# Finer first quarters, plain gain loads and later turns at the seams of a one-core encoder block

## Chip, cores and metric

The kernel runs on one core of a Trainium2 chip. The metric is device microseconds of one execution. TensorE multiplies, ScalarE and VectorE do elementwise work, GpSimd a few tiny instructions, and SyncE (SP) issues every load and store.

## The reference

One layer over x of 256 tokens by 1024 channels, float32, with an RMS norm before and after every part:

```
x = x + 0.5 * rmsnorm(swiglu(rmsnorm(x, ffn1_pre_g), w_gate, w_up, w_down), ffn1_post_g)
z = rmsnorm(x, mix_pre_g) @ w_in            # q,k,v,f | u,v_s | a_A,a_B
o_a = forgetting attention(q, k, v, f);  o_b = gelu(u) * (W_s LN(gelu(v_s)) + b)
x = x + rmsnorm((sigmoid(a_A)*o_a + sigmoid(a_B)*o_b) @ w_out, mix_post_g)
x = x + 0.5 * rmsnorm(swiglu(rmsnorm(x, ffn2_pre_g), ...), ffn2_post_g)
rmsnorm(x, g) = x * rsqrt(mean(x*x) + 1e-6) * g          # D = 1024, d_ff = 4096
```

## The kernel before

Tokens are two tiles of 128 (t = 0, 1). Every float32 operand is split into a rounded high part, made by a ScalarE copy, and the rest, the low part, made by a VectorE subtraction (`split`, L85 and L86). A product is three matmuls of 512 columns: high by high, high by low weight, low by high.

Weights come in quarters, 128x2048, of 1 MiB: column half c of 512, and half kh of the contraction. `load` brings one in (5 buffers), `parts_of` splits it (4 buffers for each part), `quarter` is both. A quarter and one token tile make a unit of 12 matmuls (`proj`). `section` goes quarter by quarter and uses each for both token tiles; `section_by_tile` keeps all four quarters, does tile 0 with them (4 units) and then tile 1. After each unit the generator yields, and `tick` runs what `later(n, ...)` put off for n ticks. FFN 1's first gate section, the mixer's v, gb and w_o, and FFN 2's first gate section go by tile. `fast` is a seven-product form for the later up sections.

A norm is `square_sum` (the sum of squares of each half), `rstd` (a sum with epsilon, and a power -0.5, on [128,1], both on GpSimd), `normed` (hn = x * r * g, VectorE) and `to_xT` (four TensorE transposes for each half, then a split into xT). `post_norm` takes the squares from PSUM, multiplies y by the gain (yg, VectorE, L186) and adds into x (L190); `pre_norm` squares x and returns a function that turns the tile later. The three seams are: the head, FFN 1's end into the mixer (done1, `after`, `turn_in`), and w_o into FFN 2 (wo_done, `before`). In FFN 1 token tile 0 is turned by `after` when KEEP f steps of 6 products for tile 1 are still to come, and tile 1 by `later(3, ...)` during v; in FFN 2 tile 0 is turned by `later(4, turn[0])` during w_o's tile 1, and tile 1 by `before` at the second step.

In the head 14 dummy matmuls run while x comes. `trace` and `in_order` fix the order of the listed instructions on each engine; elsewhere the framework orders each engine's queue at build time, by program order among what it reckons to be ready. Each engine then runs its queue in order, waiting on semaphores.

Of the kernel before, what the change touches and what calls it, by code (L numbers as in the profile page):

```python
# [22 lines left out]
P = 128  # L23
D = 1024
# [10 lines left out]
NB = 4  # L35
KEEP = 2
HOLD = 2
# [8 lines left out]
def block(ctx: ExitStack, tc: tile.TileContext, a: dict, out: bass.AP):  # L46
# [20 lines left out]
    x = const.tile([P, NT, D], F32, name="x")  # L67
    for t in range(NT):
        nc.sync.dma_start(out=x[:, t, :], in_=a["x"][t])
    xT = const.tile([P, KT, NT, 2, P], F32R, name="xT")  # L70

    ident = const.tile([P, P], F32, name="ident")
    power = const.tile([P, 4], F32, name="power")
    const.tile([P, 32], F32, name="pad1")
    nc.vector.memset(power, -0.5)

    def gain(name, by=D):
        g = gains.tile([P, D], F32, tag="g", name=f"g_{name}")
        for c in range(0, D, by):
            nc.sync.dma_start(out=g[:, c:c + by], in_=a[name][:, c:c + by].broadcast_to([P, by]))  # L80
        return g
# [32 lines left out]

    def quarter(src, name):

        return parts_of(load(src, name), name)

# [3 lines left out]
    def later(n, fn):  # L122
        pending.append([n, fn])
# [9 lines left out]

    def square_sum(srcs, name, vector=None):
        ms = small.tile([P, 2], F32, tag="ms", name=f"ms_{name}")
        for c, src in enumerate(srcs):
            if vector is not None and c == 1:
                junk = mid_tile([P, 512], f"junk_{name}{c}")
                vector.append(nc.vector.scalar_tensor_tensor(out=junk, in0=src, scalar=1.0 / D, in1=src, op0=ALU.mult,
                                                             op1=ALU.mult, accum_out=ms[:, c:c + 1]))  # L140
                continue
            junk = small.tile([P, 512], mybir.dt.bfloat16, tag="junk", name=f"junk_{name}{c}", bufs=1)
            nc.scalar.activation(out=junk, in_=src, func=AF.Square, scale=1.0 / 32.0, accum_out=ms[:, c:c + 1])
        return ms

    def rstd(ms, name, trace=None):
        r = small.tile([P, 1], F32, tag="r", name=f"r_{name}")
        done = [nc.gpsimd.tensor_scalar(out=r, in0=ms[:, 0:1], scalar1=ms[:, 1:2], scalar2=RMS_EPS, op0=ALU.add,  # L148
                                        op1=ALU.add),
                nc.gpsimd.tensor_tensor(out=r, in0=r, in1=power[:, 0:1], op=ALU.pow)]  # L150
        if trace is not None:
            trace.extend(done)
        return r
# [27 lines left out]
    def post_norm(t, ys, g, half, name):  # L181
        ms = square_sum(ys, f"{name}{t}")
        ygs = []
        for c in range(2):
            yg = mid_tile([P, 512], f"yg_{name}{t}{c}")
            nc.vector.scalar_tensor_tensor(out=yg, in0=ys[c], scalar=half, in1=halves(g)[c], op0=ALU.mult, op1=ALU.mult)  # L186
            ygs.append(yg)
        r = rstd(ms, f"{name}{t}")
        for xc, yg in zip(halves(x[:, t]), ygs):
            nc.vector.scalar_tensor_tensor(out=xc, in0=yg, scalar=r, in1=xc, op0=ALU.mult, op1=ALU.add)  # L190
# [30 lines left out]

    def section(src, name, done):

        for c in range(2):
            pss = [None, None]
            for kh in range(2):
                w = quarter(src[c, kh], f"{name}{c}{kh}")
                for i in range(2):
                    for t in range(NT):
                        if pss[t] is None:  # L230
                            pss[t] = bank(f"{name}{t}{c}")
                        proj(pss[t], t, w, kh, i, 2)
                    if kh == 1 and i == 1:
                        for t in range(NT):
                            done(t, c, pss[t])
                    yield

    def section_by_tile(src, name, done, first=None):

        ws = {}  # L240
        for t in range(NT):
            for c in range(2):
                for kh in range(2):
                    if (c, kh) not in ws:
                        ws[c, kh] = first if first and (c, kh) == (0, 0) else quarter(src[c, kh], f"{name}{c}{kh}")
                ps = bank(f"{name}{t}{c}")
                for kh in range(2):
                    proj(ps, t, ws[c, kh], kh, 0, 1)
                    if kh == 1:
                        done(t, c, ps)  # L250
                    yield
# [20 lines left out]
    def fast(src, name, parts, done):  # L272
# [6 lines left out]
        def lhs_s(i):  # L279
            return lambda k, xs: parts[:, i, k, xs, :]  # L280

# [53 lines left out]

    def ffn(n, quick, done, before=None, after=None, first=None):

# [42 lines left out]
        for b in range(NB):  # L380
            steps = []
            for src, kind, fn in ((gs[b], "g", gate_done(b)), (us[b], "u", up_done(b))):
                nm = f"{kind}{n}_{b}"
                if (b, kind) == (0, "g"):
                    steps.append((section_by_tile(src, nm, fn, first), 8))
                elif (b, kind) in quick:
                    steps.append((fast(src, nm, parts[0], fn), 7))
                else:
                    steps.append((section(src, nm, fn), 8))
# [3 lines left out]
            for gen, _ in steps:  # L393
                for _ in gen:
                    at += 1
                    if b == 0 and at == 2 and before:
                        before()
                    if b == 0 and at == 9 and quick:
                        parts.append(sums(f"f{n}"))
                    tick()  # L400
                    while had > 0 and gone < had * at // total:
                        f = side.pop(0)
                        down(f, 0)
                        down(f, 1)
                        gone += 1
# [135 lines left out]
    def mixer(turn_in):  # L541
# [4 lines left out]

        later(3, turn_in[1])
        kept = forget()
        run(section_by_tile(a["w_v"], "v", v_done))
        parts = sums("mx") if FASTM else None  # L550

# [101 lines left out]
    g = halves(gain("ffn1_pre_g", 512))  # L653
    nc.sync.dma_start(out=ident, in_=a["ident"])
    trace, rs = [], []
    for t in range(NT):
        ms = square_sum(halves(x[:, t]), f"f1{t}", vector=trace)
        rs.append(rstd(ms, f"f1{t}", trace))
    hn = {}

# [6 lines left out]

    norm_of(0, 0)
    norm_of(0, 1)
    norm_of(1, 0)  # L670
    norm_of(1, 1)
    raw = load(a["g1"][0][0, 0], "g1_0", 2)
    splits = []
    turn_of(0, 0)
    first = parts_of(raw, "g1_0", 2, splits)
    trace.extend(splits[0])
    turn_of(0, 1)
    trace.extend(splits[1])
    turn_of(1, 0)
    turn_of(1, 1)  # L680
    in_order(trace)
    turn, gs = {}, []
# [6 lines left out]

    ffn(1, FAST1, done1, after=lambda: turn[0](), first=first)  # L690
    turn = mixer(turn)
# [75 lines left out]
```

## Time and profile before

| what | value |
|---|---|
| median of 3 runs (lowest, highest) | 760.64 us (760.53, 761.41) |
| the profiled execution | 760.05 us, its span 758.3 us |
| granted TensorE clock, mean | 0.997 |
| busy: TensorE, VectorE, ScalarE | 739.0, 538.2, 381.4 us |
| DMA | 141.61 MB, mean 187 GB/s |

The span runs from the first to the last instruction of the profiled execution. Busy time of TensorE is modelled from the starts of pipelined matmuls.

### The profile page before, as it was taken

To read this page: it belongs to the slowest core of one execution; us is meant where nothing else is said; L and a number is where in the kernel's file an instruction comes from. 1 tells how busy PE (TensorE), PEld (TensorE's weight loads), DVE (VectorE), ACT (ScalarE), POOL (GpSimd) and SP (SyncE) were. 2 spreads that over 40 slices of the span, in tenths; PEclk is the share of its full clock that TensorE was granted. 3 is DMA by queue.
4 is the path that set the end of the run, shared out by engine and by line. 5 is a ranking of instruction groups with operands and counts; after the bars stand their busy time and mean duration, and the time that the engine had idled before them with its cause. 6 is when DMAs were issued, how large, how long until landed. Compare 5 with 4: busy or idle time off the path is not lost. (4 is left out here: it accounts for less than half of the span.)

```text
span 758.3 us, 8470 instructions
## 1 busy us (share of the span) xinstructions
PE 739.0 (97%) x3446; PEld 608.1 (80%) x3446; DVE 538.2 (71%) x516; ACT 381.4 (50%) x376; POOL 21.5 (3%) x32
## 2 busy tenths in 40 slices
PE   6999999999999999999999999899999999999996
PEld 3888888888888877888888888678888888888885
DVE  6584798689479775755486647848479958947972
ACT  5553465356355474754544434735346545644551
POOL 1000000000000020000020000300000000000000
PEclk9999999999999999999999999999999999999999
DMA  9785168338416936633427435527525842851521
GB/s 343 304 315 182 57 236 304 126 103 341 167 56 222 333 139 203 252 150 116 162 111 276 169 112 221 187 85 275 185 73 203 302 162 65 338 207 56 201 76 56
DMA packets 21974, 141.61 MB, mean 187 GB/s; under 512 B 3184, under 2 KB 3440, under 8 KB 5680
## 3 DMA queue, kind: packets, MB, share of 16 engines
q1 hardware_dynamic: 21936, 141.08, 50.6%
q8 instruction: 27, 0.44, 0.2%
q14 instruction: 11, 0.09, 0.0%
HBM read 140.02 MB, written 1.05 MB: 186 GB/s over the span
## 5 line engine op out<-in xcount | busy, mean ns | idle before, releaser
L219 PE MATMUL g<-hi_g,xT 128*128 128x512 f32 x512 | 164.7, 393 | 0.5 <-ACT hi_g L85 0.3
L352 PE MATMUL y<-hi_d,hT 128*128 128x512 f32 x512 | 147.4, 392 | 0.0
L219 PEld LDWEIGHTS g<-hi_g,xT 128*128 128x128 f32 x512 | 96.8, 189 | 21.1 <-ACT hi_g L85 1.1
L352 PEld LDWEIGHTS y<-hi_d,hT 128*128 128x128 f32 x512 | 95.7, 188 | 19.4
L86 DVE TENSOR_TENSOR lo_g<-raw_g,hi_g 128x2048 fp32r<-128x2048 f32 (+1 forms) x33 | 73.4, 2224 | 43.8 <-ACT hi_g L85 43.8
L219 PE MATMUL g<-lo_g,xT 128*128 128x512 f32 x256 | 100.4, 392 | 2.8 <-DVE lo_g L86 2.7
L86 DVE TENSOR_TENSOR lo_d<-raw_d,hi_d 128x2048 fp32r<-128x2048 f32 x32 | 73.0, 2286 | 36.9 <-ACT hi_d L85 36.9
L352 PE MATMUL y<-lo_d,hT 128*128 128x512 f32 x256 | 81.0, 392 | 0.0
L85 ACT CAST hi_g<-raw_g 128x2048 fp32r<-128x2048 f32 (+1 forms) x33 | 61.2, 1857 | 33.7 <-PE u L219 9.8
L85 ACT CAST hi_d<-raw_d 128x2048 fp32r<-128x2048 f32 x32 | 60.8, 1914 | 25.9 <-PE g L219 8.6
L219 PE MATMUL u<-hi_u,xT 128*128 128x512 f32 x192 | 60.6, 391 | 0.0
L219 PEld LDWEIGHTS g<-lo_g,xT 128*128 128x128 f32 x256 | 48.4, 189 | 13.5 <-DVE lo_g L86 3.8
L352 PEld LDWEIGHTS y<-lo_d,hT 128*128 128x128 f32 x256 | 47.8, 188 | 9.7
L291 DVE TENSOR_TENSOR raw_u<-raw_u,raw_u 128x2048 f32<-128x2048 f32 x24 | 55.0, 2292 | 0.8
L358 ACT ACTIVATE sg<-g 128x512 f32<-128x512 f32 x32 | 18.9, 598 | 65.4 <-PE g L219 65.4
L198 PE MATMUL qk<-xT,hi_qk 128*128 128x512 f32 x128 | 46.3, 403 | 0.0
L85 ACT CAST hi_u_3p<-raw_u 128x2048 fp32r<-128x2048 f32 x14 | 26.6, 1913 | 33.0 <-DVE raw_u L291 26.0
L219 PEld LDWEIGHTS u<-hi_u,xT 128*128 128x128 f32 x192 | 36.1, 188 | 7.4
L86 DVE TENSOR_TENSOR lo_u<-raw_u,hi_u 128x2048 fp32r<-128x2048 f32 x12 | 27.3, 2289 | 17.3 <-ACT hi_u L85 17.3
L86 DVE TENSOR_TENSOR lo_u_3p<-raw_u,hi_u_3p 128x2048 fp32r<-128x2048 f32 x14 | 31.9, 2288 | 9.4 <-ACT hi_u_3p L85 9.4
L219 PE MATMUL u<-lo_u,xT 128*128 128x512 f32 x96 | 37.4, 389 | 0.0
L85 ACT CAST hi_u_1p<-raw_u 128x2048 fp32r<-128x2048 f32 x14 | 26.8, 1917 | 20.1 <-DVE raw_u L291 9.5
(254 smaller groups left out, 1270.9 us busy)
## 6 DMA issues: line engine op xcount, KB each, us to landing
raw_u<-in_u SPq DMA_DIRECT2D x32, 1024.0 KB, 4.8
raw_d<-in_dn SPq DMA_DIRECT2D x32, 1024.0 KB, 4.7
raw_g<-in_g SPq DMA_DIRECT2D x31, 1024.0 KB, 4.8
raw_qk<-in_w_qk SPq DMA_DIRECT2D x8, 1024.0 KB, 5.4
raw_v<-in_w_v SPq DMA_DIRECT2D x4, 1024.0 KB, 5.2
raw_sv<-in_w_sv SPq DMA_DIRECT2D x4, 1024.0 KB, 4.7
raw_u<-in_w_u SPq DMA_DIRECT2D x4, 1024.0 KB, 4.8
raw_ga<-in_w_ga SPq DMA_DIRECT2D x4, 1024.0 KB, 4.7
```

The lines of the kernel that those rows point to most:

```text
L85: return [nc.scalar.copy(out=hi, in_=src), nc.vector.tensor_tensor(out=lo, in0=src, in1=hi.bitcast(F32), op=ALU.subtract)]
L86: nc.vector.tensor_tensor(out=lo, in0=src, in1=hi.bitcast(F32), op=ALU.subtract)]
L198: nc.tensor.matmul(ps, lhsT=hi, rhs=xT[:, k], start=k == 0, stop=False, skip_group_check=True)
L219: nc.tensor.matmul(ps, lhsT=xT[:, kh * 4 + k, t, xs, :], rhs=v, start=kh == 0 and k == 0 and q == 0, stop=kh == 1 and k == 3 and q == 2)
L291: nc.vector.tensor_tensor(out=out, in0=p, in1=q, op=ALU.add)
L352: nc.tensor.matmul(ys[t][c], lhsT=hTs[f // 4][:, f % 4, t, xs, :], rhs=w[:, c * 512:(c + 1) * 512], start=f == 0 and q == 0, stop=f == NF ...
L358: nc.scalar.activation(out=sg, in_=y, func=AF.Silu)
```

## The change

- The gains lie in memory as 128 equal rows and are loaded plainly; before, one row was spread over 128 partitions by the load.
- In the head: x's tile 0, the identity, the gain halves, then x's tile 1 are loaded; the first two quarters (c = 0, kh = 0 and 1) come and are split in four pieces each. FFN 1's first gate section is a `section`, so both quarters serve both tiles: quarter 0 for tile 0, then tile 1, with the second halves of both tiles turned (`within`) ahead of tile 1's last 6 matmuls. The written order of VectorE and ScalarE changes with it.
- Pre-norms share their squares: half 0 on ScalarE, half 1 on VectorE. Post-norms stay on ScalarE. The sum with epsilon moves from GpSimd to VectorE for all norms.
- Quarters of v and of FFN 2's first gate section are split in four pieces (loaded whole).
- Token tile 1 is turned one unit later in the mixer (ahead of its own first unit) and two units later in FFN 2 (likewise). KEEP is 1 instead of 2.
- `section` takes the banks of both tiles at once; `parts` is a list.

```diff
-KEEP = 2
+KEEP = 1
...
-    for t in range(NT):
-        nc.sync.dma_start(out=x[:, t, :], in_=a["x"][t])
+    nc.sync.dma_start(out=x[:, 0, :], in_=a["x"][0])
...
+    nc.sync.dma_start(out=ident, in_=a["ident"])
...
-            nc.sync.dma_start(out=g[:, c:c + by], in_=a[name][:, c:c + by].broadcast_to([P, by]))
+            nc.sync.dma_start(out=g[:, c:c + by], in_=a[name][:, c:c + by])
...
-    def quarter(src, name):
-
-        return parts_of(load(src, name), name)
+    def quarter(src, name, parts=1):
+
+        return parts_of(load(src, name), name, parts)
...
-    def square_sum(srcs, name, vector=None):
+    def square_sum(srcs, name, trace=None, shared=True):
...
-            if vector is not None and c == 1:
+            if shared and c == 1:
...
-        done = [nc.gpsimd.tensor_scalar(out=r, in0=ms[:, 0:1], scalar1=ms[:, 1:2], scalar2=RMS_EPS, op0=ALU.add,
+        done = [nc.vector.tensor_scalar(out=r, in0=ms[:, 0:1], scalar1=ms[:, 1:2], scalar2=RMS_EPS, op0=ALU.add,
                                         op1=ALU.add),
                 nc.gpsimd.tensor_tensor(out=r, in0=r, in1=power[:, 0:1], op=ALU.pow)]
...
-        ms = square_sum(ys, f"{name}{t}")
+        ms = square_sum(ys, f"{name}{t}", shared=False)
...
-    def section(src, name, done):
+    def section(src, name, done, first=None, within=None):
+
+
 
         for c in range(2):
-            pss = [None, None]
+            pss = [bank(f"{name}{t}{c}") for t in range(NT)]
             for kh in range(2):
-                w = quarter(src[c, kh], f"{name}{c}{kh}")
+                early = first and (c, kh) == (0, 0)
+                w = first[kh] if first and c == 0 else quarter(src[c, kh], f"{name}{c}{kh}")
                 for i in range(2):
-                    for t in range(NT):
-                        if pss[t] is None:
-                            pss[t] = bank(f"{name}{t}{c}")
-                        proj(pss[t], t, w, kh, i, 2)
+                    if early:
+                        for j in range(2):
+                            if (i, j) == (1, 1):
+                                within()
+                            proj(pss[i], i, w, kh, j, 2)
+                    else:
+                        for t in range(NT):
+                            proj(pss[t], t, w, kh, i, 2)
...
-                    steps.append((section_by_tile(src, nm, fn, first), 8))
+                    steps.append((section(src, nm, fn, first, within) if first else section_by_tile(src, nm, fn, 4), 8))
...
-                    if b == 0 and at == 2 and before:
+                    if b == 0 and at == 4 and before:
...
-        later(3, turn_in[1])
+        later(4, turn_in[1])
         kept = forget()
-        run(section_by_tile(a["w_v"], "v", v_done))
...
+        run(section_by_tile(a["w_v"], "v", v_done, 4))
...
-    norm_of(0, 0)
+    rs = []
+    for t in range(NT):
+        rs.append(rstd(square_sum(halves(x[:, t]), f"f1{t}", trace), f"f1{t}", trace))
+        norm_of(t, 0)
+    first = [parts_of(load(a["g1"][0][0, c], f"g1_0{c}", 4), f"g1_0{c}", 4, splits) for c in range(2)]
+    turn_of(0, 0)
+    trace.extend(splits[0])
+    turn_of(1, 0)
+    for i in splits[1:4]:
+        trace.extend(i)
     norm_of(0, 1)
-    norm_of(1, 0)
     norm_of(1, 1)
...
+    def within():
+        turn_of(0, 1)
+        trace.extend(splits[4])
+        turn_of(1, 1)
+        for i in splits[5:]:
+            trace.extend(i)
+        in_order(trace)
...
-        arrays[n] = np.ascontiguousarray(i[n].reshape(1, D))
+        arrays[n] = np.ascontiguousarray(np.broadcast_to(i[n].reshape(1, D), (P, D)))
```

## Rows read from the trace of the kernel before

**Rows 1.** The page, its span and its first part, busy time by engine.

```profile
span 758.3 us, 8470 instructions
...
PE 739.0 (97%) x3446; PEld 608.1 (80%) x3446; DVE 538.2 (71%) x516; ACT 381.4 (50%) x376; POOL 21.5 (3%) x32
```

**Rows 2.** Waits of TensorE over the span: total us, times, longest us.

```profile
PE tp_f L162 <- DVE hn_f L168: 4.7, 2, 3.5
PE g L219 <- DVE lo_g L86: 2.7, 2, 1.9
```

**Rows 3.** The chain that ended last, FFN 2: start us, us, work.

```profile
526.69 0.87 PE hp L373 x8
...
544.82 5.44 PE g L219 x24
```

**Rows 4.** Timeline of the head: start us, us, engine, line, operation, [idle before <-releaser].

```profile
5.75 0.69 DVE L139 SCALAR_TENSOR_TENSOR junk_f<-x 128x512 f32<-128x512 f32 x1 [0.96 <-DMA x<-in_x]
...
8.77 2.12 PE L162 MATMUL tp_f<-ident,hn_f 128*128 128x128 f32 x16 [1.88 <-DMA ident<-in_ident]
9.44 0.59 ACT L85 CAST xT<-tp_f 128x512 fp32r<-128x512 f32 x1 [2.90 <-PE tp_f L162]
10.10 0.68 DVE L86 TENSOR_TENSOR xT<-tp_f,xT 128x512 fp32r<-128x512 f32 x1
...
18.20 0.50 PE L219 MATMUL g<-lo_g,xT 128*128 128x512 f32 x1 [1.92 <-DVE lo_g L86]
```

**Rows 5.** Windows, products of L219 in the head: window, us, PE busy (instructions).

```profile
11.20:18.19 6.99, 4.08 (x13) 1.00 1.01 427
```

**Rows 6.** DMA of the first 20 us, in 40 slices of 0.5 us.

```profile
GB/s 0 0 0 123 229 360 426 393 401 303 213 246 176 270 281 327 290 393 418 467 434 442 410 459 426 393 459 410 410 442 426 442 442 410 459 393 410 475 410 410
```

**Rows 7.** Windows of the two seams, TensorE alone (instructions at the edges count too).

```profile
479.73:484.84 5.11, 3.96 (x21) 1.00 0.57 208
484.84:502.03 17.19, 13.69 (x57) 0.90 0.57 214
273.15:278.76 5.61, 4.04 (x22) 1.00 0.50 187
278.76:291.43 12.67, 12.11 (x57) 1.00 0.77 265
```

**Rows 8.** Windows behind the second transposes before FFN 2: PEclk is the granted clock.

```profile
494.00:498.00 4.00, 4.00 (x15) 3.23 (x16) 3.92 (x7) 1.17 (x2) 0.00 (x0) 0.57 0.63 250
```

**Rows 9.** Timeline of the seam from FFN 1 to the mixer, VectorE and GpSimd.

```profile
267.67 1.42 DVE L190 SCALAR_TENSOR_TENSOR x<-yg_p,r_p,x 128x512 f32<-128x512 f32 x2 [0.35 <-POOL r_p L150]
...
271.76 1.77 POOL L148 TENSOR_SCALAR r_mx<-ms_mx 128x1 f32<-128x1 f32 x1 [4.12 <-ACT junk_mx L143]
```

**Rows 10.** Timeline of the tail.

```profile
752.66 0.19 ACT L143 ACTIVATION_READ_ACCUMULATOR junk_p<-y 128x1 f32 x1
752.89 0.69 DVE L186 SCALAR_TENSOR_TENSOR yg_p<-y,g_ffn_post_g 128x512 f32<-128x512 f32 x1 [0.65 <-ACT junk_p L143]
752.96 0.30 POOL L148 TENSOR_SCALAR r_p<-ms_p 128x1 f32<-128x1 f32 x1 [9.44 <-ACT junk_p L143]
753.34 0.56 POOL L150 TENSOR_TENSOR r_p<-r_p,power 128x1 f32<-128x1 f32 x1
753.93 1.42 DVE L190 SCALAR_TENSOR_TENSOR x<-yg_p,r_p,x 128x512 f32<-128x512 f32 x2 [0.35 <-POOL r_p L150]
```

**Rows 11.** Instructions of the tile rl in the mixer: ns min/median/max.

```profile
L576 DVE TENSOR_SCALAR rl<-mv x4: 162/165/170, 378.7 to 396.8; 128x4 f32<-128x4 f32 x4
```

**Rows 12.** Timeline of the seam from the mixer to FFN 2, VectorE.

```profile
473.60 1.42 DVE L190 SCALAR_TENSOR_TENSOR x<-yg_pm,r_pm,x 128x512 f32<-128x512 f32 x2 [0.36 <-POOL r_pm L150]
...
480.14 1.42 DVE L168 SCALAR_TENSOR_TENSOR hn_f<-x,r_f,g_ffn_pre_g 128x512 f32<-128x512 f32 x2 [0.85 <-POOL r_f L150]
...
484.27 1.28 DVE L86 TENSOR_TENSOR xT<-tp_f,xT 128x512 fp32r<-128x512 f32 x2
```

**Rows 13.** Groups of VectorE by form, 468 to 500 us: count, busy us, mean ns.

```profile
L86 DVE TENSOR_TENSOR lo_g<-raw_g,hi_g 128x2048 fp32r<-128x2048 f32 x4 | 9.1, 2286 | 2.0 <-ACT hi_g L85 2.0
```

More of the change, by code (lines that the diff above doesn't have):

```diff
@@ L131, in tick @@
             e[1]()
-    def square_sum(srcs, name, vector=None):
+    def square_sum(srcs, name, trace=None, shared=True):
         ms = small.tile([P, 2], F32, tag="ms", name=f"ms_{name}")
         for c, src in enumerate(srcs):
-            if vector is not None and c == 1:
+            if shared and c == 1:
                 junk = mid_tile([P, 512], f"junk_{name}{c}")
-                vector.append(nc.vector.scalar_tensor_tensor(out=junk, in0=src, scalar=1.0 / D, in1=src, op0=ALU.mult,
-                                                             op1=ALU.mult, accum_out=ms[:, c:c + 1]))
+                done = nc.vector.scalar_tensor_tensor(out=junk, in0=src, scalar=1.0 / D, in1=src, op0=ALU.mult,
+                                                      op1=ALU.mult, accum_out=ms[:, c:c + 1])
+                if trace is not None:
+                    trace.append(done)
                 continue
@@ L236, in section, with section_by_tile @@
                     yield
-    def section_by_tile(src, name, done, first=None):
+    def section_by_tile(src, name, done, parts=1):
         ws = {}
@@ L244, in section_by_tile @@
                     if (c, kh) not in ws:
-                        ws[c, kh] = first if first and (c, kh) == (0, 0) else quarter(src[c, kh], f"{name}{c}{kh}")
+                        ws[c, kh] = quarter(src[c, kh], f"{name}{c}{kh}", parts)
                 ps = bank(f"{name}{t}{c}")
@@ L279, in lhs_s @@
         def lhs_s(i):
-            return lambda k, xs: parts[:, i, k, xs, :]
+            return lambda k, xs: parts[0][:, i, k, xs, :]
         def product(ps, lhs, raw, nm, start):
@@ L334, in block, with ffn @@
     marks = {}
-    def ffn(n, quick, done, before=None, after=None, first=None):
+    def ffn(n, quick, done, before=None, after=None, first=None, within=None):
         gs, us, dn = a[f"g{n}"], a[f"u{n}"], a[f"dn{n}"]
@@ L384, in ffn @@
                 if (b, kind) == (0, "g"):
-                    steps.append((section_by_tile(src, nm, fn, first), 8))
+                    steps.append((section(src, nm, fn, first, within) if first else section_by_tile(src, nm, fn, 4), 8))
                 elif (b, kind) in quick:
-                    steps.append((fast(src, nm, parts[0], fn), 7))
+                    steps.append((fast(src, nm, parts, fn), 7))
                 else:
@@ L545, in v_done @@
             nc.scalar.copy(out=v[:, t, c * 512:(c + 1) * 512], in_=ps)
-        later(3, turn_in[1])
+        later(4, turn_in[1])
         kept = forget()
-        run(section_by_tile(a["w_v"], "v", v_done))
-        parts = sums("mx") if FASTM else None
+        run(section_by_tile(a["w_v"], "v", v_done, 4))
+        parts = [sums("mx")] if FASTM else None
         def columns(src, name, done):
@@ L653, in block @@
     g = halves(gain("ffn1_pre_g", 512))
[L654 to L659, printed above, removed]
+    nc.sync.dma_start(out=x[:, 1, :], in_=a["x"][1])
+    trace, splits, hn = [], [], {}
     def norm_of(t, c):
@@ L666, in turn_of @@
         trace.extend(to_xT(t, c, hn[t, c], "f1"))
-    norm_of(0, 0)
+    rs = []
[8 more added lines that the diff above has]
+        trace.extend(i)
     norm_of(0, 1)
-    norm_of(1, 0)
     norm_of(1, 1)
[L672 to L681, printed above, removed]
+    def within():
[5 more added lines that the diff above has]
+        in_order(trace)
     turn, gs = {}, []
@@ L688, in done1 @@
         turn[t] = pre_norm(t, gs[1], "mx")
-    ffn(1, FAST1, done1, after=lambda: turn[0](), first=first)
+    ffn(1, FAST1, done1, after=lambda: turn[0](), first=first, within=within)
     turn = mixer(turn)
```

## The prediction

> **What bounds the kernel now.** I read the page's first part, then TensorE's waits, then the timeline around each wait. TensorE is busy for 97% of the span [rows 1], so only its gaps can be won, and they lie in few places. The waits say which [rows 2]: transposes waiting for a normed tile, and first weight halves in the head. Elsewhere TensorE issues one 512-column product every 0.2267 us (24 in 5.44) and one transpose every 0.11 us (8 in 0.87) [rows 3]. So I price each place by counting: time spent minus products times 0.2267 minus transposes times 0.11.
>
> *Head.* The 14th product starts at 18.20 [rows 4], 13 came before it [rows 5]: as if an unbroken run had begun at 18.20 - 13 x 0.2267 = 15.25. The page's DMA row dips to 176 to 303 GB/s between 4.5 and 7.5 us, when the gain rows are spread to 128 partitions, against 390 to 475 later [rows 6].
>
> *Seams.* Four stretches, two per seam, hold 8 transposes each plus 12 or 48 products, ideally 3.62 or 11.78 us [rows 7]. FFN 1 to mixer: 5.61 (one product more at its edge, 0.23) loses 1.76, 12.67 loses 0.89. Mixer to FFN 2: 5.11 loses 1.49, 17.19 loses 5.41. Of the 5.41, 3.5 is waiting [rows 2]; the rest is the granted clock of 0.57, between the levels 1.2 and 2.4 GHz, in the 4 us behind that wait [rows 8]. Sum 9.55.
>
> **The change part by part.**
>
> *Pre-norm chain (shared squares, adding and eps on VectorE, later turn, KEEP 1).* GpSimd's small addition took 1.77 us at 271.76 [rows 9] and 0.30 at 752.96 where VectorE was doing nothing long [rows 10]: it was held up. On VectorE it is one instruction like the 128x4 one, 0.165 us [rows 11]. The second square leaves ScalarE, and costs VectorE 0.69 beside the first [rows 4]. Each chain gets some 2 us shorter (1.6 and most of a square), and the later turns give it 1.36 us (6 products, KEEP) or 2.72 and 5.44 us more (one or two units of 12). So the waits for hn should all go, and with the 3.5 us wait the low clock.
>
> The addition now waits on VectorE for ScalarE's square, and any weight piece queued behind it waits too, with the products for it; the two squares run side by side, so that is 0.2 us a chain at most.
>
> What is late next is VectorE, because it takes on squares, additions, and quarters in four pieces. I add up what it must do from the end of x for token tile 0 until tile 1 can be turned: 2 squares 1.4; 3 additions 0.5; 4 hn 2.84, at 1.42 a pair; xT's two lows 1.28; 2 yg 1.38; x 1.42 [rows 4, 10, 11, 12]; and 16 weight pieces. A whole low part is 2.29 [rows 13]; pieces of 128x512 have the size of xT's lows, 1.28 a pair, so 0.64 each and 10.24. Sum 19.1. From 475.02 (473.60 + 1.42) that is 494.1 [rows 12], and from 269.09 (267.67 + 1.42) 288.2 [rows 9].
>
> The late turn also exposes something new. Tile 1's first product now stands right behind its transposes. In the head the first transpose began at 8.77, ScalarE's half at 9.44 (0.59 long), VectorE's at 10.10 (0.68 long, as xT's) [rows 4]: the third product, the first to need the low half, can start 2.0 us after the first transpose, against 0.87 + 0.45 = 1.3 unexposed. That is 0.7 us; with a copy of 0.59 ahead on ScalarE 1.3. I take 0.8 per seam. It needs both engines idle, which they should be: all four weight quarters are held until tile 1 has used them, so no further split can queue there.
>
> Mixer seam: TensorE's own earliest start of tile 1 is 291.43 - 1.76 - 0.89 + 0.8 = 289.6. By VectorE it is 288.2 + 0.45 (last three products; two follow a start) + 0.87 + 0.8 = 290.3. I take 290.3, a gain of 1.1. FFN 2 seam: 502.03 - 6.90 + 0.8 = 495.9 by TensorE, 494.1 + 2.1 = 496.2 by VectorE, a gain of 5.8. Bounds: without the VectorE bound 1.8 and 6.1; with the exposure of 1.3 and one weight piece ahead on each engine (1.3 more) the mixer seam loses 0.7 and the FFN 2 seam wins 4.0.
>
> *Head.* x's tile 0 comes first, then identity, gains, then tile 1: 1.64 MB stand before its last byte where 1.05 MB stood. The DMA row sums to 0.97 MB at 4.5 us; 0.67 MB more at about 400 GB/s makes 6.2, and x was usable about 1 us behind its bytes (5.75 against some 4.6) [rows 4, 6]: 7.1 where it was 5.75. At the 248 GB/s of the dip it is 8.3, at 426 6.7. From there VectorE is in a written order: square, addition, GpSimd's power 0.56, hn [rows 4, 10, 11] and hand-overs: 9.5. Then six lows (two of xT, four weight pieces) at 0.64: 13.4. Tile 0's first twelve products end 0.5 later, 13.9; six of tile 1, then the eight transposes from 15.25. VectorE begins tile 0's second low at 15.25 + 1.33 = 16.6, and the fourth from there, the second piece of quarter two, is done at 19.15. That releases the 29th product: 19.15 - 28 x 0.2267 = 12.8 instead of 15.25. I take 2.2 off, not 2.45, since a cast of a later quarter may slip into ScalarE's idle time before the second turn. Bounds: 0.4 (x at 8.3 and such a cast) and 3.2. Issues: SP now puts out eight pieces where two halves and a quarter went; its queue has room, as the DMA rate, not issue, sets the landings.
>
> The Trainium skill, "DMA: Bandwidth & Descriptors", says to batch loads to 1 MiB or more (section Bandwidth) and fits 2.0 us plus bytes over 436 GB/s to each load, measured on loads that GpSimd issues (section Anatomy of one DMA); if eight pieces paid that 2.0 + 0.6 us one behind the other, an estimate from that page, the second quarter would be whole some 21 us behind tile 1, and the sum would shrink by 7.3 us (rival 3). The rows contradict it for loads in a queue: 393 to 426 GB/s from 3 to 4.5 us while x's two tiles of 512 KB came [rows 6].
>
> *Tail.* No VectorE work competes there, so GpSimd's addition costs 0.30 [rows 10]. On VectorE it stands behind yg of the second half, which starts at 752.89: 753.6, plus 0.17, power 0.56, so x at 754.4 instead of 753.93: 0.45 lost. KEEP 1 gives the first half's square 0.68 us of head start instead of 1.36, while that square and its readout take 0.8: 0.1 lost. Together 0.55. If the addition is put ahead of yg it is 0, with KEEP twice as dear 0.7.
>
> *At nothing:* the gain loads elsewhere (the same bytes, behind weights that are loaded ahead; without that lead 512 KB at 400 GB/s would be 1.3 us each), the parts list, both banks taken at once (TensorE's unit of 6 products covers the second).
>
> **Sum.** 2.2 + 1.1 + 5.8 - 0.55 = 8.55. The profiled execution took 760.05 us (span 758.3 and 1.75 around it); 751.5. The median of the runs, 760.64, is 0.59 higher, so 752.1.
>
> **The rivals.**
> 1. *The head gives nothing.* Tile 1 lands at 8.3 or the written order stalls VectorE on a transpose. For: its chain now holds both tiles' norms ahead of the first low. Against: quarter one's products then have twice the use. Gain 6.35 at most, some 0.5 less in the seams: 754.5 (753.5 to 756).
> 2. *VectorE becomes the bound at the seams*: its 19.1 us are underestimated by idle waits for GpSimd's power, which its own pieces hold up (as the addition was [rows 9]), 1.5 to 2 us a seam. For: VectorE's sum already ends behind TensorE's. Against: pieces fill the waits. 8.55 - 3.5: 755.6 (754 to 758).
> 3. *The pieces land one behind another.* If each 256 KB paid 0.6 us for its bytes and about twice the 1 us that x lagged behind its own, 2.6 each, the eighth would land at 7.1 + 20.8 = 27.9 and be split at 29.2; its products, the 41st on, are due at 12.8 + 40 x 0.2267 = 21.9. That costs 7.3: 759.4. It decides from 1.7 us a piece on. Against it: [rows 5, 6]. The page named above would give the same.
> 4. *Slower: the late turn.* Tile 1's transposes wait for nothing, but their two copies queue behind other work on ScalarE and VectorE with TensorE idle at both seams. It needs 8.55 us, 4.3 a seam over the 0.8: two whole weight splits (2.29 each) on VectorE ahead of xT's lows. If it were three, 762.7. Against: no free weight buffers at that time.
> 5. *The chains stay as long* (additions queue on VectorE exactly as GpSimd did): the mixer seam wins nothing, but two units of 12 still cover the 3.5 us: within 756 to 758.
>
> **How the numbers follow.** My forecast 0.60, rival 1 0.14, rival 2 0.12, rival 3 0.04, rival 4 0.06, rival 5 0.04. The likeliest one's own range is 749.4 (all upper bounds: 3.2 + 1.8 + 6.1 - 0) to 755. The range reaches over rivals 1, most of 2 and half of 5: 749.4 to 757. A measurement here tells 0.2%, 1.5 us, from no change: faster is below 759.1. Rival 4 is slower in most of its share; of the others little comes within 0.2%: faster 0.90, same 0.05, slower 0.05.
>
> **What would show it.** In the profile after: no wait of a transpose for hn in the seams and full clock behind the second; TensorE's waits for xT's halves of 0.5 to 1 us in both instead; VectorE full from the end of x to the turn; an unbroken head from about 19 us; the last x starting 1.7 rather than 1.27 us behind the readout of the last square (752.66 and 753.93 before). The prediction is wrong if tile 1 of x lands after 8.3, if a weight split stands ahead of xT's lows, or if TensorE's clock falls in the head, whose products are now thinly spread.

## Result and the profile after

The changed kernel takes 755.62 us (median of four runs, 755.46 to 755.94), the kernel before beside it 761.02 (760.53 to 763.63): ratio 0.9923 [0.9899, 0.9946], 5.4 us faster. The forecast was 752.1 in a range of 749.4 to 757.0, a gain of 8.5 us. The sign and the range held, and so did most of the seams; the head did not, in these two profiles.

The page of the kernel after, span and first part:

```profile
span 753.7 us, 8526 instructions
...
PE 739.6 (98%) x3446; PEld 608.8 (81%) x3446; DVE 544.5 (72%) x565; ACT 380.0 (50%) x397; POOL 12.9 (2%) x20
```

TensorE does the same work in the same busy time as in [rows 1]; the span is 4.6 us shorter, so only gaps moved. To see where, I take marks: the first product of a name that both kernels issue in the same place of the order. Timeline of TensorE, three marks in the kernel before, not shown so far:

```profile
37.17 0.39 PE L219 MATMUL u<-hi_u,xT 128*128 128x512 f32 x1
...
304.25 0.39 PE L198 MATMUL qk<-xT,hi_qk 128*128 128x512 f32 x1
...
512.93 0.39 PE L219 MATMUL u<-hi_u,xT 128*128 128x512 f32 x1
```

The same marks in the kernel after:

```profile
37.12 0.39 PE L222 MATMUL u<-hi_u,xT 128*128 128x512 f32 x1
...
303.82 0.39 PE L201 MATMUL qk<-xT,hi_qk 128*128 128x512 f32 x1
...
507.56 0.39 PE L222 MATMUL u<-hi_u,xT 128*128 128x512 f32 x1
```

The differences are 0.05, 0.43 and 5.37, and 4.6 at the span's end. So the head won 0.05, the seam into the mixer 0.38, the seam into FFN 2 4.94, and what follows lost 0.77, nearly all in the tail.

Waits of TensorE in the kernel after (total us, times, longest us), to be set against [rows 2]:

```profile
PE tp_f L165 <- DVE hn_f L171: 3.0, 1, 3.0
...
PE g L222 <- DVE lo_g L86: 1.1, 1, 1.1
PE v L222 <- DVE xT L86: 0.6, 1, 0.6
PE g L222 <- ACT xT L85: 0.5, 2, 0.3
PE v L222 <- DVE lo_v L86: 0.3, 1, 0.3
PE v L222 <- ACT xT L85: 0.3, 1, 0.3
```

No transpose waits for hn in a seam any more. The one wait of 3.0 us for hn stands in the head. What is left in the seams are waits for VectorE's low parts (lo_g 1.1, lo_v 0.3, xT 0.6) and the exposed turns (xT from ScalarE).

*Head.* Timeline of the kernel after, all engines:

```profile
7.83 0.69 DVE L140 SCALAR_TENSOR_TENSOR junk_f<-x 128x512 f32<-128x512 f32 x1 [1.37 <-DMA x<-in_x]
...
9.54 0.75 DVE L171 SCALAR_TENSOR_TENSOR hn_f<-x,r_f,g_ffn_pre_g 128x512 f32<-128x512 f32 x1 [0.67 <-POOL r_f L153]
9.17 0.62 ACT L85 CAST hi_g<-raw_g 128x512 fp32r<-128x512 f32 x1
...
10.35 1.11 PE L165 MATMUL tp_f<-ident,hn_f 128*128 128x128 f32 x4 [3.00 <-DVE hn_f L171]
...
18.15 1.03 PE L165 MATMUL tp_f<-ident,hn_f 128*128 128x128 f32 x8
...
22.25 0.39 PE L222 MATMUL g<-lo_g,xT 128*128 128x512 f32 x1
```

x's tile 1 was usable at 7.83 (forecast 7.1, bounds 6.7 to 8.3), and its hn ran from 9.54 to 10.29 (forecast 9.5 for its end). The first weight piece was cast from 9.17, but TensorE's queue has the transposes of tile 1 ahead of the first product, so it stood still for 3.0 us. Then its clock was low. Window 11 to 16.5 us of the kernel after, all engines (us, busy of PE, PEld, DVE, ACT and POOL, granted clock, DMA share, GB/s):

```profile
11.00:16.50 5.50, 5.25 (x14) 3.84 (x13) 5.48 (x9) 2.14 (x4) 0.00 (x0) 0.50 1.05 428
```

TensorE is busy 5.25 of 5.50 us and issues 14 instructions: at the lower of its two levels, 1.2 GHz, products follow each other every 0.43 us (three from 12.72 to 14.01) instead of every 0.2267. The product at 22.25 is the 32nd: as if an unbroken run had begun at 22.25 - 31 x 0.2267 = 15.22, where it was 15.25.

*Seam into FFN 2.* Window where [rows 8] showed 0.57, and VectorE, GpSimd and TensorE before it, kernel after:

```profile
494.00:498.00 4.00, 3.71 (x19) 2.95 (x20) 3.17 (x6) 1.57 (x3) 0.00 (x0) 1.00 0.61 217
```

```profile
473.67 1.42 DVE L193 SCALAR_TENSOR_TENSOR x<-yg_pm,r_pm,x 128x512 f32<-128x512 f32 x2 [0.73 <-POOL r_pm L153]
...
490.95 0.86 POOL L153 TENSOR_TENSOR r_f<-r_f,power 128x1 f32<-128x1 f32 x1 [3.53 <-DVE r_f L151]
...
493.19 1.29 DVE L86 TENSOR_TENSOR lo_g<-raw_g,hi_g 128x512 fp32r<-128x512 f32 x2
493.92 0.50 PE L222 MATMUL g<-lo_g,xT 128*128 128x512 f32 x1 [1.10 <-DVE lo_g L86]
```

Clock 1.00 where it was 0.57. VectorE's last piece ends at 493.19 + 1.29 = 494.5 (forecast 494.1, on the time of the kernel before; this kernel was 0.43 us ahead by then). Behind the turn TensorE waits 0.29 us for xT from ScalarE, and its third product starts 1.90 us behind the first transpose.

*Tail.* Timeline of the kernel after, against [rows 10]:

```profile
747.30 0.19 ACT L146 ACTIVATION_READ_ACCUMULATOR junk_p<-y 128x1 f32 x1
...
748.13 0.20 DVE L151 TENSOR_SCALAR r_p<-ms_p 128x1 f32<-128x1 f32 x1
748.48 0.55 POOL L153 TENSOR_TENSOR r_p<-r_p,power 128x1 f32<-128x1 f32 x1 [9.94 <-DVE r_p L151]
749.06 1.41 DVE L193 SCALAR_TENSOR_TENSOR x<-yg_p,r_p,x 128x512 f32<-128x512 f32 x2 [0.73 <-POOL r_p L153]
```

From readout to x it is 1.76 us (forecast 1.7), where it was 1.27.

### The profile page after: what moved, and what is told of

It reads as the page before. It is cut to its first block, busy times and chain, and to the rows that moved or that the text cites. A ratio compares the mean times of both kernels' runs of the same rounds, so it can differ in the third digit from the quotient of the medians.

```text
span 753.7 us, 8526 instructions
## 1 busy us (share of the span) xinstructions
PE 739.6 (98%) x3446; PEld 608.8 (81%) x3446; DVE 544.5 (72%) x565; ACT 380.0 (50%) x397; POOL 12.9 (2%) x20
## 4 chain that ended last, share of the span: by engine, by line
PE 91%; DVE 4%; issue 1%; POOL 1%; ACT 1%; DMA 1%; SPq 0%; POOLq 0%; DVEq 0%; ACTq 0%
PE g L222 22%; PE y L362 22%; PE u L222 9%; PE qk L201 4%; PE sv L222 3%; PE ga L222 3%; PE gb L222 3%; PE qk L202 2%; PE hp L383 2%; PE v L222 2%; PE u_3D L297 1%; PE u_1C L297 1%; PE u_1D L297 1%; PE u_2C L297 1%; PE wo L222 1%; PE u_2D L297 1%
## 5 line engine op out<-in xcount | busy, mean ns | idle before, releaser
L362 PEld LDWEIGHTS y<-hi_d,hT 128*128 128x128 f32 x512 | 95.7, 188 | 19.4
L86 DVE TENSOR_TENSOR lo_g<-raw_g,hi_g 128x2048 fp32r<-128x2048 f32 (+1 forms) x50 | 75.0, 1520 | 42.0 <-ACT hi_g L85 42.0
L85 ACT CAST hi_g<-raw_g 128x2048 fp32r<-128x2048 f32 (+1 forms) x50 | 62.8, 1292 | 32.8 <-PE u L222 9.3
L85 ACT CAST hi_u_2p<-raw_u 128x2048 fp32r<-128x2048 f32 x14 | 26.9, 1918 | 20.1 <-DVE raw_u L301 9.5
```

What stands on the lines that cost most here:

```text
L85: return [nc.scalar.copy(out=hi, in_=src), nc.vector.tensor_tensor(out=lo, in0=src, in1=hi.bitcast(F32), op=ALU.subtract)]
L86: nc.vector.tensor_tensor(out=lo, in0=src, in1=hi.bitcast(F32), op=ALU.subtract)]
L362: nc.tensor.matmul(ys[t][c], lhsT=hTs[f // 4][:, f % 4, t, xs, :], rhs=w[:, c * 512:(c + 1) * 512], start=f == 0 and q == 0, stop=f == NF ...
```

## The experiments

Each ratio is to the kernel before on the same chip. The marks above, taken in every run's trace, say in which place each kernel won or lost; us gained on the profile of before in each place:

| kernel | head | seam to mixer | seam to FFN 2 | rest |
|---|---|---|---|---|
| the change | 0.05 | 0.38 | 4.94 | -0.77 |
| 1 old head | -0.68 | 0.42 | 4.96 | -0.50 |
| 2 filled wait | 2.17 | 0.42 | 4.98 | -0.67 |
| 3 x first | 2.51 | 0.34 | 4.98 | -0.73 |
| 4 KEEP 2 | 1.07 | 0.29 | 5.00 | -0.66 |
| 5 turns alone, on before | -0.67 | -0.40 | 4.83 | 0.04 |
| 6 old turns | 0.66 | 0.74 | 0.03 | -0.73 |
| 7 whole quarters | 0.98 | 1.52 | 3.82 | -0.72 |
| 8 squares apart | 0.06 | 1.20 | 5.23 | -0.79 |
| 9 longer warm-up, on before | -1.33 | 0.00 | 0.04 | 0.09 |
| 10 rstd before yg | 0.86 | 0.86 | 5.77 | -0.19 |
| 11 first sum | 1.84 | 1.32 | 6.11 | -0.07 |
| 12 second sum | 3.74 | 1.30 | 6.10 | -0.04 |

Where two kernels have the same code in a seam, its column agrees within about 0.1 us. The head's does not: six executions of the changed head (the change, 4, 6, 7, 8, 10) give 0.05 to 1.07, mean 0.61, and three of the old one (before, 1, 5) give 0, -0.68 and -0.67. So kernels are compared in the seams by this table, not by their times alone.

For the head the times say more than these single profiles. The profile of before is a good draw: 47 of the 48 other executions on record took longer than its 760.05 us. Take the median of before on the same chip, less a kernel's median, less what the table gives its two seams and the rest: that leaves 0.85 to 3.10 us for the head of the six kernels with the changed head (mean 2.06), and -0.29 and 0.79 for runs 1 and 5, which have the old one (mean 0.25). It is an estimate that takes the seams of before to repeat, as they do in run 9 (0.00 and 0.04).

**1. Old head.** The changed kernel, with the loads, norms and weight parts of the head as before (an excerpt of the edit).

```diff
-    nc.sync.dma_start(out=x[:, 0, :], in_=a["x"][0])
+    for t in range(NT):
+        nc.sync.dma_start(out=x[:, t, :], in_=a["x"][t])
...
-    first = [parts_of(load(a["g1"][0][0, c], f"g1_0{c}", 4), f"g1_0{c}", 4, splits) for c in range(2)]
+    raw = load(a["g1"][0][0, 0], "g1_0", 2)
+    first = parts_of(raw, "g1_0", 2, splits)
```

> The changed kernel with the head of before (load order, spread gain load in the head, order of VectorE, FFN 1's first gate section by tile); seams and tail as changed. Theory Q, the new head won nothing because TensorE waited 3.0 us at tile 1's transposes and then ran at low clock: 755.6 us, as the changed kernel, within 0.4. Rival H, the head won the 2.2 us as forecast and some other place lost them: 757.8.

Measured: 757.39 (755.86 to 759.07), 0.9936 [0.9921, 0.9952]. It lies between the two theories, 0.4 us from rival H and 1.8 from theory Q, but its interval overlaps that of the change, and its executions spread over 3.2 us, of which the profile is the fastest. On the same chip run 4, which has the new head, took 755.37. By the table's nine profiles the new head is worth some 1 us (0.61 against a mean of -0.45), by the medians some 1.8 (2.06 against 0.25): not 0, and by the medians not far from 2.2.

**2. The wait in the head filled.** 24 transposes, whose result nothing reads, keep TensorE busy between the transposes of tile 0 and of tile 1.

```diff
+FILL = 24
...
+    for i in range(FILL):
+        nc.tensor.transpose(out=warm[:, 0:P], in_=hn[0, 0][:, i % 4 * P:i % 4 * P + P], identity=ident)
```

> The changed kernel with 24 dummy transposes of tile 0's normed half between the first two real groups of transposes; they fill the 3.0 us wait with work whose output nothing reads. Theory Q: the granted clock stays at 1.0 from 11 to 16.5 us and the run takes about 2 us less than the changed kernel, 753.5, though every wait for data stays. Rival V, VectorE's written order sets the head's pace and the clock costs nothing: 755.6.

Measured: 753.12 (753.01 to 753.34), 0.9882 [0.9868, 0.9896]. Timeline of the head of this kernel, and its window (TensorE alone):

```profile
7.11 2.78 PE L682 MATMUL warm<-ident,hn_f 128*128 128x128 f32 x24
...
10.62 0.66 PE L166 MATMUL tp_f<-ident,hn_f 128*128 128x128 f32 x4 [0.72 <-DVE hn_f L172]
...
20.12 0.39 PE L223 MATMUL g<-lo_g,xT 128*128 128x512 f32 x1
```

```profile
11.00:16.50 5.50, 5.19 (x26) 1.00 1.04 417
```

Tile 1 is turned even later than in the kernel after (10.62 against 10.35), yet the clock is 1.00 and the 32nd product starts 2.1 us sooner. So the head's loss is the clock behind the wait, not the wait.

**3. x first.** Both tiles of x ahead of identity and gains, both means before the normed halves.

```diff
-    nc.sync.dma_start(out=x[:, 0, :], in_=a["x"][0])
+    for t in range(NT):
+        nc.sync.dma_start(out=x[:, t, :], in_=a["x"][t])
...
-    nc.sync.dma_start(out=x[:, 1, :], in_=a["x"][1])
...
-        norm_of(t, 0)
+    norm_of(0, 0)
+    norm_of(1, 0)
```

> The changed kernel with both tiles of x loaded ahead of the identity and the gains, and both tiles' squares ahead of both normed halves in the written order. Theory Q: tile 1's transposes come 1.5 us earlier, TensorE is idle for some 1.5 us instead of 3.0 and keeps its clock: 752 to 753.5. Rival V: 755 to 755.6, as the weight pieces and VectorE set the pace.

Measured: 752.88 (751.44 to 753.14), 0.9875 [0.9859, 0.989]. Timeline and window of the head:

```profile
8.13 1.32 PE L166 MATMUL tp_f<-ident,hn_f 128*128 128x128 f32 x8 [1.03 <-DVE hn_f L172]
```

```profile
11.00:16.50 5.50, 5.50 (x23) 0.77 1.04 426
```

Both tiles are turned at 8.13, and the head wins about as much as by filling the wait (2.51 and 2.17). The run doesn't part its two causes: the turn came earlier, and the clock was higher than in the kernel after. It was still partly low (0.77), although TensorE had waited only 1.03 us, so theory Q's time was met, but not its clock.

**4. KEEP 2.** Twice as many products kept back for the time behind the transposes.

```diff
-KEEP = 1
+KEEP = 2
```

> The changed kernel with KEEP 2 again. Theory K, KEEP 1 turns tile 0 so late that v's third product waits for xT's low half (0.58 us) and the tail's squares are 0.1 later: 754.9, 0.7 to 0.8 less than the changed kernel. Rival, KEEP 1 is what keeps TensorE from waiting for hn of tile 0: the wait of before comes back in part, 755.6 or more.

Measured: 755.37 (754.43 to 755.75), 0.9912 [0.9897, 0.9927]. Timeline of its seam into the mixer:

```profile
286.50 0.50 PE L222 MATMUL v<-lo_v,xT 128*128 128x512 f32 x1 [1.03 <-DVE lo_v L86]
```

v's wait for xT's low part is gone, as theory K had it, but the wait for lo_v grew from 0.34 to 1.03: the table's seam is the same (0.29 for 0.38). VectorE's sum sets that seam, and KEEP only chooses where TensorE waits for it. The 1 us by which this profile is shorter than that of the change arose in the head.

**5. The later turns alone, on the kernel before.**

```diff
-                    if b == 0 and at == 2 and before:
+                    if b == 0 and at == 4 and before:
...
-        later(3, turn_in[1])
+        later(4, turn_in[1])
```

> The kernel before with one edit: tile 1 is turned where the changed kernel turns it (one unit later in the mixer, two in FFN 2). Theory T, the later turns win the FFN 2 seam's second gap (5.41 us, with the low clock) at the price of 0.7 us of exposed copies in each seam: 756.5 to 757.5, the waits of tile 0 (1.6 and 1.2 us) staying. Rival C, the shorter norm chain is what won: above 760.

Measured: 756.83 (756.24 to 758.91), 0.9933 [0.9914, 0.9951]. As theory T had it, the turns alone win 4.83 of the 4.94 us at the seam into FFN 2, and lose 0.40 at the seam into the mixer, where no wait of tile 1 for hn was there to be saved and the exposed turn is pure cost. The waits for tile 0's hn (1.6 and 1.2 us) stay. The old head of this profile ran at low clock. Its window, TensorE alone:

```profile
11.00:16.50 5.50, 5.03 (x14) 0.50 1.01 427
```

**6. The changed kernel with the old turns**, the reverse of 5.

> The changed kernel with tile 1 turned where the kernel before turned it. Theory T: tile 1's chain is no shorter than before (9.7 us from w_o's last product to hn against 8.8), so a transpose waits about 4 us again ahead of FFN 2 and the clock falls behind it: 760 to 761. Rival C: the chain is short enough and the two exposures of 0.6 to 0.8 us go: 754.5 to 756.

Measured: 759.71 (758.38 to 760.58), 0.9964 [0.9952, 0.9977]. Its timeline at the seam into FFN 2:

```profile
491.75 1.94 PE L165 MATMUL tp_f<-ident,hn_f 128*128 128x128 f32 x8 [4.22 <-DVE hn_f L171]
```

The wait for tile 1's hn is 4.22, longer than the 3.5 before: the reworked chain of tile 1 is not shorter. The seam wins 0.03.

**7. Quarters split whole** in v and FFN 2's first section.

```diff
-                    steps.append((section(src, nm, fn, first, within) if first else section_by_tile(src, nm, fn, 4), 8))
+                    steps.append((section(src, nm, fn, first, within) if first else section_by_tile(src, nm, fn, 1), 8))
...
-        run(section_by_tile(a["w_v"], "v", v_done, 4))
+        run(section_by_tile(a["w_v"], "v", v_done, 1))
```

> The changed kernel with the quarters of v and of FFN 2's first gate section split whole instead of in four pieces. VectorE then has 1.2 us less to do at each seam (9.0 instead of 10.24 for the low parts). Theory V, VectorE's sum bounds the seams: up to 1 us faster in each, 754 to 755. Rival P, the pieces are what lets the norms of tile 1 through between them: an hn later by up to 2 us, 756.5 to 758.

Measured: 755.52 (754.46 to 756.75), 0.9914 [0.9894, 0.9933]: no different. The table shows why, each theory held at one seam: whole splits win 1.14 at the mixer and lose 1.12 before FFN 2. Timeline at the second:

```profile
485.32 2.28 DVE L86 TENSOR_TENSOR lo_g<-raw_g,hi_g 128x2048 fp32r<-128x2048 f32 x1
485.55 2.46 POOL L153 TENSOR_TENSOR r_pm<-r_pm,power 128x1 f32<-128x1 f32 x1 [10.71 <-DVE r_pm L151]
```

GpSimd's small power, begun 0.23 us into a whole split, took 2.46 us instead of 0.55.

**8. Squares apart.** The seams' pre-norm squares both on ScalarE again.

```diff
-        r = rstd(square_sum(halves(x[:, t]), f"{name}{t}"), f"{name}{t}")
+        r = rstd(square_sum(halves(x[:, t]), f"{name}{t}", shared=False), f"{name}{t}")
```

> The changed kernel with both squares of the seams' pre-norms on ScalarE again (the head's stay shared). VectorE has 1.4 us less to do at each seam. Theory V: the waits for the last weight pieces (1.10 us in FFN 2, 0.34 in the mixer) shrink, 754.5 to 755.3. Rival, the square stands on ScalarE behind weight casts and tile 0's hn comes too late again: 756 to 757.

Measured: 754.34 (753.62 to 755.24), 0.9895 [0.9876, 0.9914]. The wait for lo_v is gone and that for lo_g 0.9; the seams win 0.82 and 0.29 more than with the change. Sharing the squares costs 1.1 us in the two seams, since it puts 0.69 us a chain on the engine that sets both seams.

**9. A longer warm-up, on the kernel before**: WARM 14 to 18.

> The kernel before with 18 dummy products ahead of the head's transposes instead of 14, which fill TensorE's idle time until the identity has come (the results are not read). Theory Q2, the old head too runs at low clock in some executions and its 1.0 in the profile of before was a good one: the clock stays at 1.0 from 11 to 16.5 us, the runs lie close together, 760.0 to 760.6, 1 to 1.5 below the median of before on the same chip. Rival, the old head always keeps its clock: as before.

Measured: 762.63 (760.9 to 763.64), 1.0003 [0.999, 1.0017]; the times still spread over 2.7 us (4.0 for the kernel before). Timeline of its head, VectorE, and its window, TensorE alone:

```profile
9.51 2.08 DVE L168 SCALAR_TENSOR_TENSOR hn_f<-x,r_f,g_ffn_pre_g 128x512 f32<-128x512 f32 x3 [1.33 <-DMA g_ffn_pre_g<-in_ffn_pre_g]
```

```profile
11.00:16.50 5.50, 5.50 (x23) 0.70 1.02 430
```

Half of the theory held: the old head too runs at low clock in some executions, 0.70 here and 0.50 in run 5. Its remedy fell: here the gain row landed late, hn waited 1.33 us for it (0.21 in the profile of before) and TensorE 3.66 us for hn, and work ahead of the wait does not fill it. Nor is the clock what holds the old head back: its 14th product starts at 18.90 us in run 1, at a clock of 1.00, and in run 5, at 0.50, alike, and even in run 5 TensorE had waited 0.75 us for VectorE's lo_g by then.

**10. rstd ahead of yg.** The post-norm's addition is issued on VectorE before the product with the gain.

```diff
-        ms = square_sum(ys, f"{name}{t}", shared=False)
+        r = rstd(square_sum(ys, f"{name}{t}", shared=False), f"{name}{t}")
...
-        r = rstd(ms, f"{name}{t}")
```

> The changed kernel with the addition of the post-norms ahead of yg in the program, so that on VectorE it no longer stands behind yg of the second half. Theory: the tail gets back what yg cost it, the last x starts 1.2 us behind the readout of the last square instead of 1.7, 0.5 us less in all: 755.1. Rival, yg of the second half is then late itself and x waits for it: no change, 755.6.

Measured: 752.83 (752.53 to 753.39), 0.9877 [0.9855, 0.9899]. Timeline of its tail:

```profile
745.27 0.19 ACT L146 ACTIVATION_READ_ACCUMULATOR junk_p<-y 128x1 f32 x1
745.50 0.21 DVE L151 TENSOR_SCALAR r_p<-ms_p 128x1 f32<-128x1 f32 x1
745.63 0.68 DVE L189 SCALAR_TENSOR_TENSOR yg_p<-y,g_ffn_post_g 128x512 f32<-128x512 f32 x1
...
746.44 1.42 DVE L192 SCALAR_TENSOR_TENSOR x<-yg_p,r_p,x 128x512 f32<-128x512 f32 x2
```

x starts 1.17 us behind the readout instead of 1.76. The kernel gains more than was expected, since the post-norms feed the seams too: 0.48, 0.83 and 0.58 us at the mixer, FFN 2 and the rest, 1.9 in all. The other 0.8 us of this profile is the head's scatter.

**11. First sum**: 2, 4, 8 and 10 together.

> The changed kernel with the edits that helped: dummy transposes in the head, the seams' squares on ScalarE, KEEP 2, the post-norm's addition ahead of yg. If they add up (2.5 for the clock, 1.0 to 1.3 for VectorE, 0.5 for the tail, up to 0.4 for KEEP): 751.2. If KEEP 2 only moves the wait to VectorE again: 751.6.

Measured: 750.68 (750.52 to 750.87), 0.9847 [0.9826, 0.9869].

**12. Second sum**: 3, 4, 8 and 10, with WARM 17 and 7 transposes, whose result nothing reads, behind those of tile 1.

> As the run before, but with x's tile 1 ahead of the gains, 17 dummy products ahead of the transposes and 7 dummy transposes behind them. The head then begins its unbroken run some 0.4 us earlier than with the dummies alone (12.7 against 13.1) or earlier still if the clock stays at 1.0: 750.3 to 750.8. Rival, VectorE and the landing of the weight pieces bind: 751.2.

Measured: 749.17 (748.95 to 749.40), 0.9827 [0.9806, 0.9849], faster than both kernels, and 1.1 us below the lower end of what was expected. Timeline and window of its head:

```profile
8.09 1.32 PE L167 MATMUL tp_f<-ident,hn_f 128*128 128x128 f32 x8 [1.32 <-DVE hn_f L173]
...
18.52 0.44 PE L223 MATMUL g<-lo_g,xT 128*128 128x512 f32 x1
```

```profile
11.00:16.50 5.50, 5.50 (x30) 1.00 1.05 428
```

Start-equivalent 18.52 - 31 x 0.2267 = 11.5: an early turn and a full clock together give the head 3.7 us, more than the upper bound of 3.2 that the forecast set.

## Why the prediction was right or wrong

The forecast was 8.55 us off the profile of before, and the profile after is 4.6 shorter. The 3.95 that are missing stand in the head (2.15), in the seams (0.7 and 0.9) and in the tail (0.2).

**Head, forecast 2.2: the step that failed** is "six of tile 1, then the eight transposes from 15.25": they started at 18.15. The forecast priced the head by VectorE's order, with TensorE at full clock throughout. But in TensorE's queue the transposes of tile 1 stand ahead of the first product, so it waited 3.0 us for tile 1's hn, and the clock fell, which the prediction named as a way to be wrong and did not price. In run 2, with the clock full and x's tile 1 no earlier, the start-equivalent is 20.12 - 31 x 0.2267 = 13.1 where 12.8 was forecast: the rest of the step was nearly right. (There the transposes started at 16.03.) The six executions of the changed head agree: the two whose clock was 0.50 and 0.51 gained 0.05 and 0.06 us, the four at 0.69 to 0.71 gained 0.66 to 1.07.

The base was a single draw too: the profile of before has the best of three executions of the old head, with a clock of 1.00. By the means of the profiles the change wins about 1 us there, by the medians about 1.8. That this is near the forecast 2.2 is luck: the new head lost its clock, and the usual old head is slower than the one the sum began from. In these two profiles the outcome is that of rival 1, which had 754.5. Its late landing did not come (7.83, not 8.3). VectorE did stall on a transpose, as its other reason says, 2.87 us ahead of 19.40; but in run 2, with the same written order and the clock full, that was 0.59, so most of it followed from TensorE's clock.

**Seam into the mixer, forecast 1.1, measured 0.38.** VectorE's sum was right in size: from the end of x, 269.53, to that of the last low part, 288.71, it is 19.2 us, forecast 19.1. In part that is luck, since three waits of 0.44 us for GpSimd's power were not in the sum, and pieces that follow each other start 0.60 apart where 0.64 was taken. What the forecast left out is that x itself ends later. The post-norm's addition stands behind yg here as it does in the tail; its 0.45 was priced in the tail alone, and here x ends 0.44 later than before (269.09). Then TensorE takes 0.72 us from VectorE's end to the first transpose, where 0.45 was taken. The two make up the missing 0.7. The wait for tile 0's hn went. Timeline of the kernel after, VectorE and TensorE:

```profile
267.25 0.20 DVE L151 TENSOR_SCALAR r_p<-ms_p 128x1 f32<-128x1 f32 x1
268.11 1.42 DVE L193 SCALAR_TENSOR_TENSOR x<-yg_p,r_p,x 128x512 f32<-128x512 f32 x2 [0.66 <-POOL r_p L153]
...
273.84 3.70 DVE L86 TENSOR_TENSOR lo_v<-raw_v,hi_v 128x512 fp32r<-128x512 f32 x6
277.45 1.28 DVE L86 TENSOR_TENSOR xT<-tp_mx,xT 128x512 fp32r<-128x512 f32 x2
278.19 0.74 PE L222 MATMUL v<-hi_v,xT 128*128 128x512 f32 x2 [0.58 <-DVE xT L86]
...
287.42 1.29 DVE L86 TENSOR_TENSOR lo_v<-raw_v,hi_v 128x512 fp32r<-128x512 f32 x2
```

The forecast also overlooked the order in front of tile 0's low halves: six weight pieces stand ahead of xT's lows, and TensorE waits 0.58. This is the "weight split ahead of xT's lows" of the prediction, as pieces. It is not what the seam lost: run 4 shows it to be the same bound seen in another place, since without that wait the same time is lost at lo_v.

**Each chain some 2 us shorter: true for tile 0 alone.** From the end of x to the start of hn tile 0 takes 2.98 and 2.57 us in the two seams, 5.12 before; tile 1 takes 2.99 and 2.98, 3.04 before. Timeline of VectorE in the kernel after, around the power at 490.95 shown above:

```profile
490.00 0.69 DVE L86 TENSOR_TENSOR lo_g<-raw_g,hi_g 128x512 fp32r<-128x512 f32 x1
490.60 0.21 DVE L151 TENSOR_SCALAR r_f<-ms_f 128x1 f32<-128x1 f32 x1
490.73 0.68 DVE L86 TENSOR_TENSOR lo_g<-raw_g,hi_g 128x512 fp32r<-128x512 f32 x1
```

A weight piece stands between the square, which ended at 490.08, and the addition (0.6 us), and another beside the power, which took 0.86 instead of 0.55. Run 6 shows the result: with the old turns tile 1's hn comes later than before the change. What made that wait go is the later turn, as run 5 shows; rival 5 described tile 1's chains correctly.

**Seam into FFN 2, forecast 5.8, measured 4.94.** The mechanism was right: no wait for hn, full clock. The term was 0.9 too large for the same reasons as at the mixer. x ended at 475.09 (473.67 + 1.42) in a kernel that was 0.43 us ahead by then, where 475.02 was taken: 0.5 late. The sum from there was 19.4 (to 494.48) for 19.1, and from VectorE's end to the first transpose it was 0.72 again for 0.45; the exposed turn was 0.2 cheaper than the 0.8 taken. TensorE's wait of 1.10 us for lo_g is where this shows, and no further loss. So rival 2's bound was there, VectorE ending 0.6 and 0.8 us late at the two seams instead of 1.5 to 2. Its reason, idle waits for the power, came too (0.44 to 0.46 us, three a seam), but dearly priced pieces covered them; the late x it did not name. Run 10, which puts the addition ahead of yg, gives 0.48 and 0.83 back. Together with run 8, which takes the squares off VectorE, and KEEP 2 it brings the seams to 1.3 and 6.1 (run 12), a little more than the forecast had given them.

**Tail, forecast -0.55, measured about -0.8.** The addition behind yg cost 0.49 from readout to x as forecast; run 10 gives 0.59 back. The 0.1 for KEEP did not come: the last readout follows the third mark by 239.74 us, 239.73 before. The last 0.3 lies behind x (3.23 us from its end to the span's, 2.95 before), at the store, and its cause is open.

**Rivals 3 and 4** didn't occur: in the head's window the loads came at 428 GB/s, and the exposed turn cost 0.7 and 0.6 us (the third product starts 2.05 and 1.90 us behind the first transpose, 1.32 unexposed) where 0.8 was forecast. At the mixer seam, though, the turn was moved for nothing (run 5: -0.40; run 6, with the old turn: 0.74 instead of 0.38).

**Open.** What lands x and the gain row earlier or later from execution to execution was not settled. The changed head waited 2.8 to 3.1 us in each of its six executions, yet the clock from 11 to 16.5 us was 0.50 or 0.51 in two of them and 0.69 to 0.71 in four. The store's 0.3 us at the end and the plain loads of the gains, which were not tried alone, are open too. A kernel with the old turn in the mixer seam and the later one before FFN 2 was not run.

## What to carry to other kernels

Write down each engine's queue in its real order before pricing a start: what stands ahead of the first product decides it, and an idle TensorE there can be paid a second time through its clock: here filling the wait with idle transposes won nearly as much as turning earlier (2.17 and 2.51 us), and the two together 3.74. When an instruction moves in a helper, price it at every place that calls the helper: the addition behind yg was priced in the tail and paid in both seams. Take the base of such a sum from more than one execution. Delay a tile's turn only where a wait for it was measured; elsewhere the exposed turn is pure cost. Once an off-path engine has become the bound of a seam, moving work onto it or reordering waits around it wins nothing, and small additions that release another engine belong ahead of its long work.

## What the runs showed of the hardware

- TensorE's clock was 0.50 (the level of 1.2 GHz) from 11 to 16.5 us after a wait of 3.0 us in the head, and stayed at 1.00 in run 2, where dummy transposes left waits of 0.69 and 0.72. The length of the last wait alone doesn't tell it: behind the transposes' wait it was 0.77 after 1.03 us (run 3) and 1.00 after 1.32 (run 12), 0.50 after 2.1 (run 5) and 1.00 after 2.6 (run 1).
- What a low clock cost depended on who set the pace: 2.1 us between the changed head and run 2, where the products stood behind TensorE; in the old head TensorE at 0.50 still waited 0.75 us for VectorE (run 5).
- GpSimd's 128x1 power took 0.55 us with VectorE free, 0.86 beside a piece of 0.69 and 2.46 beside a split of 2.28: it ended 0.40 and 0.41 us behind them. The Trainium skill, "SBUF — State Buffer", section "SBUF: two separate sides", says that the port pair shared by VectorE and GpSimd is an exclusive lock: a VectorE instruction with two SBUF inputs, against a GpSimd one that reads SBUF, gets it for the whole instruction if it starts first, and the other is blocked. These rows, of subtractions with two inputs in SBUF that started 0.22 and 0.23 us ahead of the power, agree with it. Beside yg, one of whose inputs is in PSUM, the power took 0.55 us (run 10, at 745.86, with yg from 745.63 to 746.31).
- The 128x1 addition took 0.20 to 0.22 us on VectorE, not the 0.165 of the 128x4 one in [rows 11].
